# Key and query projections of a transformer layer by seven half-size products in place of eight, with modulation columns moved to other stages

## The chip, the cores and the metric

The kernel runs on one core of a Trainium2 chip. The metric is device time in microseconds for one execution of the whole program; the time of a kernel is the median of several runs. The profile shows one execution, with five engines: TensorE (PE, with its weight loads shown apart as PEld), VectorE (DVE), ScalarE (ACT), GpSimd (POOL) and SyncE (SP), which here only issues DMAs.

## The reference

One encoder layer, on 512 tokens of 1024 features in float32. Every token-wise product is followed by a gated addition to the residual stream `x`.

```python
mod = silu(c) @ w_mod + b_mod                       # 9 x 1024 values
(sh1, sc1, g1, sh2, sc2, g2, sh3, sc3, g3) = split(mod)

h = modulate(rmsnorm(x, norm_ffn1), sh1, sc1)
x = x + 0.5 * g1 * swiglu(h, w_ffn1_in, w_ffn1_out) # hidden width 2816

h = modulate(rmsnorm(x, norm_mix), sh2, sc2)        # one h for both mixers
qa, ka, va, qb, kb, vb, ga, gb = split(h @ w_in)
qa, ka = rope(rmsnorm(qa)), rope(rmsnorm(ka))       # 8 and 2 heads of 64
ya = window_gqa_sink(qa, ka, va, sink) @ w_branch_a # attention A, |i-j| <= 128
qb, kb = rope(rmsnorm(qb)), rope(rmsnorm(kb))       # 4 heads x 2 maps of 64, 512 columns each
ob = diff_attention(qb, kb, vb, lam)                # attention B, dense; vb 512 columns
yb = (rmsnorm(ob, subln) * 0.8) @ w_branch_b
x = x + g2 * ((sigmoid(ga) * ya + sigmoid(gb) * yb) @ w_out)

h = modulate(rmsnorm(x, norm_ffn2), sh3, sc3)
x = x + 0.5 * g3 * swiglu(h, w_ffn2_in, w_ffn2_out)
```

## The kernel before

**High and low parts.** Every fp32 operand of a matmul is split into two fp32r parts: `high`, a cast on ScalarE, and `low`, the difference, on VectorE (`split_from`, line 190). A product of two operands is three matmuls: high by high, high by low, low by high (`mm3`, lines 174 to 176). Weights arrive in a `raw`, `u` or `b` tile through SP's DMA queue and are split into one of five `high`/`low` slots (`high_low`). There are three loaders: `load_split` (cast on ScalarE, low part on VectorE), `load_halves` (the same in two halves), and `load_main`, which makes the low part without VectorE: ScalarE writes the negated high part as `low` in two passes (line 1134) and an accumulating DMA from POOL's queue adds the weight to it (line 1135).

**Stages in order.** First SwiGLU (0 to about 340 us of the profile), the boundary in which the norm and `h` for the mixers are made (`boundary`, `hidden`, lines 354 to 363) beside three gate products, projections of values, keys and queries of attention B (`project`, lines 1202 to 1204), two more gate products, projections for attention A (`project_pairs`, lines 1222 to 1224), attention B, attention A, the two branches (`branch`), the output product, the second SwiGLU.

**Seven products for eight.** In both SwiGLUs a 2 x 2 block product of weights and activations is made by seven block products (`Unit`): the sums of weight blocks are formed in place by accumulating DMAs on POOL's queue (line 513), the sums of activation blocks by `h_sum` on VectorE, and the products are combined in `after` on VectorE (lines 538, 543, 546) and copied on ScalarE (line 536). A `Unit` names its products s1, a11, a12, s2, s4, s3 and a22; each has 24 matmuls of 256 columns at a depth of four blocks of 128 (`two`, lines 458 to 460). `ASK` and `MAKE` say how many products ahead a weight is loaded and split. The PSUM banks are x (a11, s2, s3, a22), v (s1, s4) and w (a12). `run_items` goes through a list of products, in order.

The projections of keys and queries don't use this before the change: each is four blocks of 128 tokens x 8 blocks of 128 features x 3 matmuls of 512 columns, with the activations as the stationary operand.

**Modulation columns.** The nine vectors of `mod` (G1, SC2, SH2, G2, SC3, SH3, G3 after the first two) are made 128 values at a time: a load of 512 KB of `w_mod` (line 245) and a pass of VectorE with an accumulator (`mod_col`, line 283). `column` works through lists of them: 24 in `rest`, beside the first SwiGLU (`side1`, with a credit of `SIDE` for each product), 24 in `later`, beside the value, key and query projections and two gates (`beside`, one for every `LATER` steps), and eight in `latest`, beside the output product. Columns of `later` are loaded into small `u` tiles.

**Order of the work.** In the SwiGLUs the order of instructions on SP and POOL is the program's; at the boundaries that of PE, VectorE and ScalarE. Between the value projection and the end of the branches a scheduler orders each engine's queue by its own estimate, by priority and readiness, and a planner (`Line`) puts pieces of the two attentions among the gate products and projections: each piece has a due time, worked out from estimated costs (`line.helped`), and conditions. Keys and queries are copied (`raws`), normed and rotated (`head_stats`, `rope`, lines 1256 to 1274 and 1317, with a power on POOL at line 1261), turned by four PE transposes a block (`turn_heads`, line 1281), and split. Gate products fill PE until attention B is done, the rest of them and the first branch while attention A goes on.

## Time and profile before

| what | us |
|---|---|
| median of three runs | 1034.86 (1034.34 to 1039.34) |
| the profiled execution, its own time | 1034.51 |
| its span, first to last instruction | 1032.7 |
| PE busy / VectorE / ScalarE / POOL | 1027.6 / 787.4 / 582.1 / 161.8 |

The granted clock is 0.999 of full speed over the whole span. PE's busy time counts modelled ends of overlapping matmuls, so what a matmul costs is read from the distance between two starts. An engine's idle time matters only where PE waits for it. A timeline row gives start and duration in us, the engine, the line, the operation, output and inputs; a row of groups gives count, busy us and mean ns, then the idle time ahead of the group.

### The profile page before, as it was taken

To read this page: it belongs to the slowest core of one execution; us is meant where nothing else is said; L and a number is where in the kernel's file an instruction comes from. 1 tells how busy PE (TensorE), PEld (TensorE's weight loads), DVE (VectorE), ACT (ScalarE), POOL (GpSimd) and SP (SyncE) were. 2 spreads that over 40 slices of the span, in tenths; PEclk is the share of its full clock that TensorE was granted. 3 is DMA by queue.
4 is the path that set the end of the run, shared out by engine and by line. 5 is a ranking of instruction groups with operands and counts; after the bars stand their busy time and mean duration, and the time that the engine had idled before them with its cause. 6 is when DMAs were issued, how large, how long until landed. Compare 5 with 4: busy or idle time off the path is not lost.

```text
span 1032.7 us, 18848 instructions
## 1 busy us (share of the span) xinstructions
PE 1027.6 (100%) x7346; PEld 949.0 (92%) x7346; DVE 787.4 (76%) x1457; ACT 582.1 (56%) x1013; POOL 161.8 (16%) x189
## 2 busy tenths in 40 slices
PE   9999999999999999999999999999999999999998
PEld 7889899899998998899888888989999999999998
DVE  7886667567787679859772588976898777877877
ACT  6755335244454443668785856525877556655553
POOL 1101110110100100543323101001112112212210
PEclk9999999999999999999999999999999999999999
DMA  9977887967875459796737944974498998989974
GB/s 363 371 207 202 239 241 219 251 153 243 218 188 158 144 213 410 237 281 135 181 79 185 259 136 151 367 250 103 93 239 195 238 236 209 222 228 215 207 158 113
DMA packets 70233, 220.39 MB, mean 213 GB/s; under 512 B 8448, under 2 KB 13184, under 8 KB 70144
## 3 DMA queue, kind: packets, MB, share of 16 engines
q1 hardware_dynamic: 47808, 146.52, 39.2%
q0 software_dynamic: 19200, 68.17, 35.9%
q10 hardware_dynamic: 3136, 4.51, 1.2%
q8 instruction: 57, 0.93, 0.4%
q14 instruction: 32, 0.26, 0.1%
HBM read 208.94 MB, written 10.23 MB: 212 GB/s over the span
## 4 chain that ended last, share of the span: by engine, by line
PE 96%; DVE 2%; ACT 2%; issue 0%; POOL 0%; DVEq 0%; ACTq 0%
PE acc L460 7%; PE acc L459 7%; PE acc L458 7%; PE sc L460 6%; PE sc L458 6%; PE sc L459 6%; PE sc L174 5%; PE sc L176 5%; PE sc L175 5%; PE acc L174 5%; PE acc L176 5%; PE acc L175 5%; PE tp L1281 2%; PE acc L709 2%; PE acc L1203 2%; PE acc L1202 2%
## 5 line engine op out<-in xcount | busy, mean ns | idle before, releaser
L190 ACT CAST high<-raw 128x1024 fp32r<-128x1024 f32 (+2 forms) x176 | 158.4, 914 | 149.4 <-PE sc L175 40.8
L190 DVE TENSOR_TENSOR low<-raw,high 128x1024 fp32r<-128x1024 f32 (+2 forms) x176 | 183.5, 1052 | 40.4 <-ACT high L190 38.8
L459 PE MATMUL acc<-b,high 128*128 128x256 f32 x508 | 140.5, 277 | 0.1
L458 PE MATMUL acc<-b,high 128*128 128x256 f32 x508 | 140.6, 277 | 0.0
L460 PE MATMUL acc<-b,low 128*128 128x256 f32 x508 | 140.5, 277 | 0.0
L460 PE MATMUL sc<-b,low 128*128 128x256 f32 x500 | 138.0, 276 | 0.0
L458 PE MATMUL sc<-b,high 128*128 128x256 f32 x500 | 138.0, 276 | 0.0
L459 PE MATMUL sc<-b,high 128*128 128x256 f32 x500 | 138.0, 276 | 0.0
L190 ACT CAST high<-u 128x1024 fp32r<-128x1024 f32 (+1 forms) x73 | 75.4, 1034 | 52.3 <-PE sc L175 20.0
L190 DVE TENSOR_TENSOR low<-u,high 128x1024 fp32r<-128x1024 f32 (+1 forms) x73 | 87.7, 1201 | 21.5 <-ACT high L190 20.0
L174 PE MATMUL sc<-b,high 128*128 128x512 f32 (+1 forms) x272 | 97.4, 358 | 0.0
L175 PE MATMUL sc<-b,high 128*128 128x512 f32 (+1 forms) x272 | 97.0, 357 | 0.0
L176 PE MATMUL sc<-b,low 128*128 128x512 f32 (+1 forms) x272 | 97.0, 357 | 0.0
L459 PEld LDWEIGHTS acc<-b,high 128*128 128x128 f32 x508 | 95.4, 188 | 0.5 <-DVE b L1903 0.3
L458 PEld LDWEIGHTS acc<-b,high 128*128 128x128 f32 x508 | 95.4, 188 | 0.2
L460 PEld LDWEIGHTS acc<-b,low 128*128 128x128 f32 x508 | 95.4, 188 | 0.1
L460 PEld LDWEIGHTS sc<-b,low 128*128 128x128 f32 x500 | 93.9, 188 | 0.0
L458 PEld LDWEIGHTS sc<-b,high 128*128 128x128 f32 x500 | 93.9, 188 | 0.0
L459 PEld LDWEIGHTS sc<-b,high 128*128 128x128 f32 x500 | 93.9, 188 | 0.0
L174 PE MATMUL acc<-b,high 128*128 128x512 f32 (+1 forms) x240 | 89.2, 372 | 0.0
L176 PE MATMUL acc<-b,low 128*128 128x512 f32 (+1 forms) x240 | 86.6, 361 | 0.0
L175 PE MATMUL acc<-b,high 128*128 128x512 f32 (+1 forms) x240 | 86.5, 360 | 0.0
(400 smaller groups left out, 2717.9 us busy)
## 6 DMA issues: line engine op xcount, KB each, us to landing
u<-w_mod SPq DMA_DIRECT2D x38, 512.0 KB, 8.0
b<-w_mod SPq DMA_DIRECT2D x32, 512.0 KB, 5.5
raw<-w2i SPq DMA_DIRECT2D x31, 512.0 KB, 5.6
u<-w2i POOLq DMA_DIRECT2D x31, 512.0 KB, 6.8
raw<-w1u SPq DMA_DIRECT2D x24, 512.0 KB, 6.5
u<-w1u POOLq DMA_DIRECT2D x24, 512.0 KB, 7.1
raw<-w1o SPq DMA_DIRECT2D x24, 384.0 KB, 4.8
raw<-w_gate SPq DMA_DIRECT2D x16, 512.0 KB, 5.4
```

Of the source, the lines that this page charges most:

```text
L174: PE.matmul(out, wh, xh, start=first, stop=False)
L175: PE.matmul(out, wh, xl, start=False, stop=False)
L176: PE.matmul(out, wl, xh, start=False, stop=last)
L190: last = S.copy(hi, src), V.tensor_tensor(lo, src, f(hi), ALU.subtract)
L458: PE.matmul(out, wh[:, s], xh, start=first and j == 0, stop=False, skip_group_check=True)
L459: PE.matmul(out, wh[:, s], xl, start=False, stop=False, skip_group_check=True)
L460: PE.matmul(out, wl[:, s], xh, start=False, stop=last and j == 1, skip_group_check=True)
L709: PE.matmul(out1[i][:, r], w[:, i * P : (i + 1) * P], h[:, r], start=first and r.start == 0, stop=last and r.stop == T, skip_group_check=True,
L1202: PE.matmul(out[t][:, 0:n], hh[k][:, ht], wh[:, o : o + n], start=k == 0, stop=False)
L1203: PE.matmul(out[t][:, 0:n], hh[k][:, ht], wl[:, o : o + n], start=False, stop=False)
L1281: PE.transpose(tp[:, j * P : (j + 1) * P], src, ident)
```

## The change

1. **Keys and queries by seven products.** `project` is left for the values only. `projected` makes a `Unit` for the keys and one for the queries, with `two_turned`: activations stationary, 256 columns of weights moving. The boundary's `hidden` writes, as one more ScalarE activation for each block and half, the fp32 value of `h`, of which `h_sum` makes four sums after the boundary, beside the value projection. `after` combines under a high priority. Each unit yields four quarters (256 tokens x 256 columns), which are normed and rotated by `two_blocks`, the helper of attention A, and turned four blocks at once. `item_steps` gives the planner a step for every six matmuls; the last query product a22 follows s3, with the load of gate 3 put ahead.
2. **Columns.** `rest` has 30 (credit 0.36, none at some of the last items), `later` 5 beside the value, key and query projections, and a new list `tail` 13, from the end of attention B's turns on, one for every third step of the gate products, in `u` tiles, each load after a gate's load in SP's queue. For them `silu(c)` is loaded again into a `raw` tile.
3. **The first branch's weights** are loaded by `load_split` in place of `load_main`.

The core of the diff:

```diff
-EARLY, NEXT, SIDE, LATER = 3, 3, 0.27, 4
+FIRST_BLOCK, BESIDE_V, SIDE, LATER = 30, 5, 0.36, (6, 14, 2)
...
         if value is not None:
...
-            S.activation(value, t3, AF.Identity, bias=s)
+            S.activation(value, t, AF.Identity, bias=s)
...
-                h = hidden(rs, c, sc, sh, hh[c], hl[c], r)
+                value = hq[f"b{c // 4 + 1}{n}"][:, c % 4 * H : (c % 4 + 1) * H]
+                h = hidden(rs, c, sc, sh, hh[c], hl[c], r, value)
...
+    def two_turned(po, w, k, x, first, last, js=range(2)):
+        (wh, wl), (xh, xl) = w, x
+        s = slice(k * 2 * P, (k + 1) * 2 * P)
+        for j in js:
+            r = slice(j * P, (j + 1) * P)
+            out = po[:, j * H : (j + 1) * H]
+            PE.matmul(out, xh[:, r], wh[:, s], start=first and j == 0, stop=False, skip_group_check=True)
+            PE.matmul(out, xl[:, r], wh[:, s], start=False, stop=False, skip_group_check=True)
+            PE.matmul(out, xh[:, r], wl[:, s], start=False, stop=last and j == 1, skip_group_check=True)
...
+    at = FIRST_BLOCK, FIRST_BLOCK + BESIDE_V, 6 * NC
+    rest, later, tail, latest = rest[: at[0]], rest[at[0] : at[1]], rest[at[1] : at[2]], rest[at[2] :]
...
+    def projected(w, post, odd):
+        u = Unit([w[i] for i in range(4)], 4, h1_operand, post, odd)
+        u.srcs = dict(zip(("a11", "a12", "a21", "a22"), u.srcs))
+        u.products, u.aside, u.urgent = two_turned, -ASIDE, True
+        u.in_order = ("s1", "s2", "s3", "s4", "a22")
+        return u
...
+    def keys_b(c, v, u):
+        n, i, raw = quarter(c, v)
+        rs = small(8)
+        y = two_blocks(raw, 4, table["kb"], i, rs.rearrange("p (t h) -> p t h", t=2), False)
+        y3 = y.rearrange("p (h d) -> p h d", d=HD)
+        V.tensor_tensor(y3, y3, rs.unsqueeze(2).broadcast_to([P, 8, HD]), ALU.mult)
+        def turn():
+            turn_quarter(y, n, i, kb_h, kb_l)
+            keys_done.add((n, i))
+        line.at(line.helped(3.2, 5.0) + SLACK, turn, ("tp",))
...
-        yield from beside(project(vb_w, T, values_b), LATER)
-        yield from beside(project(a["w_kb"], T, keys_b), LATER)
-        yield from beside(project(a["w_qb"], T, queries_b), LATER)
-        yield from beside(gates(lambda: gate_next[0] < EARLY_A), 1)
+            with tc.issue_after(split[0]), tc.issue_after(split[1]):
+                k.prepare("s1")
+            h_sum("n1", False)
+            for t in ("n2", "t3", "t4"):
+                h_sum(t, False)
...
+            yield from beside(project(vb_w, T, values_b, also), LATER[0])
+            items = [(k, p, None, None) for p in ("s1", "a11", "a12", "s2", "s4", "s3")]
+            items += [(q, "s1", None, None), (k, "a22", None, None)]
+            items += [(q, p, None, None) for p in ("a11", "a12", "s2", "s4")]
+            items += [(q, "s3", None, lambda: soon_gates.update({3: load_main(a["w_gate"][3], holder=3)})), (q, "a22", None, None)]
+            yield from beside(item_steps(items, MM3), LATER[1])
+            yield from beside(gates(lambda: gate_next[0] < EARLY_A), LATER[2])
...
-        yield from gates(lambda: done["b"] < NT)
+        place = sbuf("raw", [P, 1024], F32, RAW)
+        def ended():
+            if turns["b"] == 4 * NT and cact[0] is not place:
+                cact[0] = place
+                with tc.issue_after(loaded[0]):
+                    nc.sync.dma_start(place, c_scr.partition_broadcast(P))
+            return turns["b"] == 4 * NT
+        yield from beside(gates(lambda: done["b"] < NT), 3, tail, ended)
         line.drain(lambda: done["b"] == NT)
         start_a()
-        yield from gates()
+        yield from beside(gates(), 3, tail, ended)
+        while tail or asked:
+            column(tail)
...
-        yield from branch(a["w_yb"], 8, ob_h, ob_l, then_a, load_main)
+        yield from branch(a["w_yb"], 8, ob_h, ob_l, then_a, load_split)
```

More of the change, by code (lines that the diff above doesn't have):

```diff
@@ L530, in after, with combine @@
         def after(self, q):
+            self.done.add(q)
+            with tc.high_priority() if self.urgent else nullcontext():
+                rest = list(self.combine(q))
+            for c, v in rest:
+                self.post(c, v, self)
+        def combine(self, q):
             v, b = self.v, self.bank
-            self.done.add(q)
             if q in ("a11", "s1", "s2"):
@@ L575, in run_items @@
                 also()
-            u.multiply(q, ks)
+            if cost is None:
+                u.multiply(q, ks)
+                yield
+            else:
+                for k in range(u.depth):
+                    u.multiply(q, [k])
+                    yield cost
             if ks is None or u.depth - 1 in ks:
@@ L600, in h_operand, with h_sum @@
         return t[:, k, T1], t[:, k, T2]
-    def h_sum(t):
+    def h_sum(t, spare=True):
         p, q = SUMS[t]
         hq[t] = hq[q if t in ("t3", "t4") else p]
-        h_op[t] = [u4() for _ in range(2)] if t == "n1" else b8()
+        spare = spare and t == "n1"
+        h_op[t] = [u4() for _ in range(2)] if spare else b8()
         for i in range(2):
@@ L955, in item1 @@
     def item1(u, q, ks=None):
-        items1.append((u, q, ks, side1))
-    credit, asked = [0.0], []
+        pause = ks is not None if isinstance(u, Out1) else u.p == NH - 1 and q in ("s3", "s4", "a22")
+        items1.append((u, q, ks, lambda: side1(0.0 if pause else SIDE)))
+    credit, asked, summed, loaded = [0.0], [], [], []
     room = b8(F32).rearrange("p a b -> p (a b)")
@@ L1226, in project_pairs, with beside @@
         then(out)
-    gate_next = [3]
-    def beside(steps, every, columns=later):
-        for i, cost in enumerate(steps):
-            if (columns or asked) and i % every == every - 1:
+    gate_next, soon_gates = [3], {}
+    def beside(steps, every, columns=later, when=lambda: True):
+        i = 0
+        for cost in steps:
+            i += when()
+            if (columns or asked) and i % every == every - 1 and when():
                 column(columns)
@@ L1335, in values_b, with queries_b, turn @@
             line.helped(0.6)
-    def queries_b(ps):
-        queries(ps, table["qb"], rqb, qb_h, qb_l, lambda: diff_scores(0, 0))
-        for t in range(NT):
-            V.tensor_scalar(nrqb[:, t, :], rqb[:, t, :], -1.0, None, ALU.mult)
+    def queries_b(c, v, u):
+        n, i, raw = quarter(c, v)
+        rs = rqb[:, 2 * i : 2 * i + 2, 4 * n : 4 * n + 4]
+        y = two_blocks(raw, 4, table["qb"], i, rs, True)
+        V.tensor_scalar(nrqb[:, 2 * i : 2 * i + 2, 4 * n : 4 * n + 4], rs, -1.0, None, ALU.mult)
+        def turn():
+            turn_quarter(y, n, i, qb_h, qb_l)
+            queries_done.add((n, i))
+            if (n, i) == (0, 0):
+                line.at(
+                    line.free["tp"] + SLACK, lambda: diff_scores(0, 0), SCORES + (lambda: len(keys_done) == 4,)
+                )
+        line.at(line.helped(2.6, 5.0) + SLACK, turn, ("tp",))
     head_b = {}
```

146 lines of the change are left out of this document (66 added, 80 removed).

## The prediction

> **What bounds the kernel now.** I read the page first, then the waits of PE, then busy time by stage, then the single matmuls. Page, engines and the chain that ended last:
>
> ```profile
> span 1032.7 us, 18848 instructions
> PE 1027.6 (100%) x7346; PEld 949.0 (92%) x7346; DVE 787.4 (76%) x1457; ACT 582.1 (56%) x1013; POOL 161.8 (16%) x189
> PE 96%; DVE 2%; ACT 2%; issue 0%; POOL 0%; DVEq 0%; ACTq 0%
> ```
>
> All waits of PE that the profile names:
>
> ```profile
> PE acc L634 <- DVE sm L640: 0.9, 1, 0.9
> PE acc L187 <- DVE u L190: 0.2, 1, 0.2
> ```
>
> TensorE is the bound, and nothing waits in front of it: 1.1 us in all. So the kernel's time is the sum of the matmuls' spacings, and a change is worth what it takes out of that sum less the waits that it makes. What the other engines have free is read by stage (columns: length; busy us and count of PE, PEld, DVE, ACT, POOL; clock; DMA share; GB/s):
>
> ```profile
> 75.00:316.00 241.00, 241.00 (x1717) 225.00 (x1717) 173.74 (x242) 106.91 (x140) 26.06 (x30) 1.00 0.78 213
> 346.00:374.00 28.00, 28.00 (x236) 27.83 (x235) 21.44 (x48) 15.95 (x29) 3.64 (x6) 1.00 0.18 58
> 374.00:396.00 22.00, 22.00 (x99) 18.20 (x98) 16.75 (x29) 4.97 (x10) 0.00 (x0) 1.00 1.01 389
> 396.00:418.00 22.00, 22.00 (x99) 18.23 (x98) 19.33 (x38) 7.93 (x16) 0.00 (x0) 1.00 1.03 409
> 418.00:440.00 22.00, 22.00 (x102) 18.18 (x102) 20.45 (x42) 15.55 (x30) 13.19 (x8) 1.00 0.65 199
> 545.00:570.00 25.00, 25.00 (x133) 21.04 (x132) 5.70 (x13) 12.85 (x30) 6.46 (x11) 1.00 0.79 197
> 570.00:640.00 70.00, 69.84 (x449) 59.12 (x448) 54.29 (x184) 49.72 (x125) 5.68 (x8) 1.00 0.61 182
> ```
>
> The rows are the first SwiGLU, the boundary to the mixers, the projections of values, keys and queries (22 us each), the end of attention B, and attention A. VectorE is nearly full in the three projections and nearly idle at the end of B.
>
> **The products.** Spacing of one projection matmul today, 512 columns wide: 13 steps from the first row to the last.
>
> ```profile
> 395.85 0.39 PE L1204 MATMUL acc<-high,b 128*128 128x512 f32 x1
> ...
> 398.79 0.39 PE L1202 MATMUL acc<-high,b 128*128 128x512 f32 x1
> ```
>
> 2.94 / 13 = 0.226 us. Keys and queries are 2 x 4 blocks x 8 k x 3 = 192 of them: 43.5 us. Seven products of 4 k x 2 halves x 3 make 168 matmuls per projection, 336 in all, each 256 wide. What does one cost? Four stretches of 256-wide matmuls, first and last row of each:
>
> ```profile
> 369.77 0.28 PE L175 MATMUL acc<-b,u 128*128 128x256 f32 x1
> ...
> 373.49 0.28 PE L176 MATMUL acc<-b,u 128*128 128x256 f32 x1
> ...
> 451.27 0.28 PE L1222 MATMUL acc<-high,b 128*128 128x256 f32 x1
> ...
> 456.99 0.28 PE L1223 MATMUL acc<-low,b 128*128 128x256 f32 x1
> ...
> 488.05 0.28 PE L1223 MATMUL acc<-low,b 128*128 128x256 f32 x1
> ...
> 488.84 0.28 PE L1224 MATMUL acc<-high,b 128*128 128x256 f32 x1
> ...
> 899.73 0.28 PE L459 MATMUL sc<-b,high 128*128 128x256 f32 x1
> ...
> 901.89 0.28 PE L460 MATMUL sc<-b,low 128*128 128x256 f32 x1
> ```
>
> 31 steps of 0.120 (weights in a u tile), 49 of 0.117 and 7 of 0.113 (attention A's projections, with activations as the stationary operand, the form the change uses), 19 of 0.114 (second SwiGLU). So 336 of them cost 38.0 to 40.3 us; I take the middle of the two A rows, 0.115, the nearest form: 38.6 us. The gain is 43.5 - 38.6 = 4.9 us, between 3.2 and 5.5. Sixteen transposes per projection stay sixteen.
>
> The Trainium skill, TensorE: Matmul & The Clock Gate, section Back-to-back issue gap, speaks against this: in streams of weight load and matmul it gives about 81 ns at 128 columns and 131 ns at 512, so half the width would cost clearly more than half. By that rule, interpolated (an estimate), 256 columns cost about three quarters of 512 and the change would lose some 14 us. The rows above show half, 0.115 against 0.226, and they decide.
>
> **What is added on VectorE and ScalarE.** Mean durations (busy us, mean ns):
>
> ```profile
> L190 DVE TENSOR_TENSOR low<-raw,high 128x1024 fp32r<-128x1024 f32 x104 | 126.5, 1223 | 28.8 <-ACT high L190 27.2
> L283 DVE CUSTOM_DVE_ANT_0 u<-u,ka,begin 128x1024 f32<-128x1024 f32 x8 | 10.3, 1283 | 6.1 <-DMA u<-w_mod 4.5 <-PE sc L1203 1.6
> L190 DVE TENSOR_TENSOR b<-f,b 128x512 fp32r<-128x512 f32 x22 | 15.1, 689 | 5.7 <-ACT b L190 5.7
> L1273 DVE TENSOR_TENSOR f<-f,raw 128x256 f32<-128x256 f32 x16 | 6.2, 421 | 0.0
> L355 ACT ACTIVATE b<-f,mod 128x256 fp32r<-128x256 f32 x16 | 7.9, 507 | 4.9 <-DVE f L354 4.9
> L1261 POOL TENSOR_TENSOR sm<-sm,half 128x8 f32<-128x8 f32 x4 | 9.9, 2482 | 61.1 <-DVE sm L1260 61.1
> u<-w2i POOLq DMA_DIRECT2D x31, 512.0 KB, 6.8
> ```
>
> *Boundary.* Sixteen more activations (the fp32 value of each half of h): 16 x 0.51 = 8.1 us on ScalarE, which goes from 16 to 24 of 28 us. The last low part of h comes at
>
> ```profile
> 367.53 0.48 DVE L363 SCALAR_TENSOR_TENSOR b<-f,mod,b 128x256 fp32r<-128x256 f32 x1 [0.18 <-ACT b L355]
> ```
>
> and PE needs it nine gate matmuls before 373.49 + 0.12, at about 372.5: 4.5 us of slack. A lateness of 1 to 2 us is hidden; the cover gone, it would cost what exceeds 4.5. Taken as 0.1 (bounds 0 and 2).
>
> *Value projection (22 us).* VectorE gets four sums (8 subtractions, 8 low parts, 16 x 0.69 = 11.0), three weight splits (3.7), five columns (6.4); with the values' four low parts (2.8) 24 us by row means. Queue starts lie about 0.08 closer than durations, so it just fits; only the first sum is needed when keys begin. Cost 0 (bound 1).
>
> *Keys and queries.* Eleven weight splits (13.5), six additions that combine products (4.1), and per quarter the norm and rotation: four or, for keys, five whole passes (the reduction, two products or sums, the keys' scaling, the low part after the turn) and two half ones, 4 x 0.69 + 2 x 0.42 = 3.6 or 4.3, in all 31.6. With the two late columns about 51 us against 38.6 us of products. Before it was 40 of 44, many of the moved columns among them. The excess of some 12 us spills over, as rotations can, into the next two gates (48 matmuls x 0.226 = 10.9 us of PE work that needs no VectorE). What cannot wait are the weights. A product's 24 matmuls last 2.8 us. From preparing s2 to using s4 there are five products, 13.8 us; the path is a cast and low part (2.3), an accumulating load (0.9 issue, perhaps behind a 2.5 us power on POOL, 6.8 to land), and a cast and low part again: 12.3 to 14.8. So it is just in time or about 1 us late, once per projection, and more if a rotation is ahead of it in VectorE's queue; gate 3, whose weights are loaded early, can be pulled forward. I take 1.2 us of waits in all (bounds 0 and 8.8, two waits of a whole quarter's rotation).
>
> *End of the queries.* The product a22 follows s3 in the same bank, so it must wait for VectorE's addition. The same order stands at the end of the first SwiGLU:
>
> ```profile
> 317.21 0.28 PE L460 MATMUL acc<-b,low 128*128 128x256 f32 x1
> ...
> 317.68 0.28 PE L174 MATMUL sc<-b,high 128*128 128x256 f32 x1
> 318.00 0.50 PE L174 MATMUL acc<-b,high 128*128 128x512 f32 x1
> 318.34 0.39 PE L175 MATMUL acc<-b,high 128*128 128x512 f32 x1
> 318.58 0.28 PE L458 MATMUL acc<-b,high 128*128 128x256 f32 x1
> ```
>
> There 1.37 us pass from s3's last to a22's first matmul, filled with other products but for about 0.3 us (the steps of 0.32 and 0.34 against 0.11 and 0.23). I take 0.3; bounds 0 and 1.3.
>
> **The moved columns.** Six go into the first SwiGLU: 7.7 us on a VectorE with 67 us free, 3 MB on queues at 78%: 0. Thirteen (16.7 us) go to the end of attention B, where VectorE has 19 of 25 us free; beside them the low parts of four branch tiles (4.9 us) enter attention A, where it has 16 of 70 free, while ScalarE loses two passes per tile and POOL's queue four accumulating loads. Their 13 loads stand on SP's queue among the gates': 6.8 MB on top of 197 GB/s x 25 us = 4.9 MB is 11.7 MB, 29 us at the 409 GB/s of the key stage. So loads can come late by some 3 us in all, ahead of gates that are fetched early: I take 0.2 (bounds 0 and 3). The earlier start of attention B that fewer columns allow is worth nothing by itself: matmuls of gates and branches fill all gaps already.
>
> **Sum.** -4.9 + 0.1 + 1.2 + 0.3 + 0.2 = -3.1 us. The profiled execution took 1034.51 us, its span 1032.7; the median shown is 1034.86, 0.35 above. 1034.51 - 3.1 = 1031.4 for a profiled execution; the products are regular work and I lean a little to less waiting, since nowhere else does this order of seven products show a wait: 1031.3 us.
>
> **Rivals.**
> *VectorE becomes the bound of keys and queries (slower).* If rotations stand ahead of weight splits in its queue and the gates are not pulled forward, PE takes VectorE's 51 us instead of 38.6: +12.4 - 4.9 = +7.5, 1042 us. For it: 20.45 of 22 us busy in the query stage already, POOL's power of 2.5 us in the same chain. Against: no wait of PE on a weight today. It decides from 4.9 us of waits on. The Trainium skill, SBUF — State Buffer, section Who interferes with whom, has VectorE and GpSimd share a port pair; that would lengthen POOL's part further, and no row here isolates it.
> *Weight loads set the pace (slower).*
>
> ```profile
> L1222 PEld LDWEIGHTS acc<-high,b 128*128 128x128 f32 x96 | 18.1, 188 | 0.8 <-issue 0.7
> ```
>
> Unhidden, 336 x 0.188 = 63.2 us, +19.7: 1054 us. The spacing of 0.115 in just these rows speaks against it.
> *The full gain.* 0.113 a matmul and no wait: -5.5, 1029.1 to 1029.4 us.
> *The gain is eaten.* 0.120 a matmul saves 3.2, and 2 to 4 us of waits take it: 1033.5 to 1035.5 us.
>
> **How the numbers follow.** A difference of 0.5%, 5.2 us, is about what a measurement of this kernel can tell from no change. Chances: the sum 0.53, the gain eaten 0.19, the full gain 0.14, VectorE the bound 0.12, weight loads 0.02. The full gain passes 1029.7 (half a per cent) in most of its cases: faster 0.13. Of VectorE as the bound, the worse part passes 1040: slower 0.11 with the weight loads. The rest, 0.76, is no change that can be told. The range 1029.0 to 1037.0 leaves out the worse part of the VectorE case, the weight loads and a little below.
>
> **What would show it.** Right: in the key and query stage 336 matmuls 256 wide at 0.113 to 0.117; fewer PE instructions of 512 columns by 192; VectorE near full there and busy at the end of B; PE still at 100% with waits under 3 us. Wrong: PE waits on low parts L190 or on the copies of the combined products, or on gate loads at the end of B; spacing of 0.12 and more; a gap before the first value matmul.

## The result, and the profile after

The changed kernel takes 1064.84 us (median of four, 1062.81 to 1069.71) against 1035.04 for the kernel before in the same session: a ratio of 1.0294, 95% interval 1.0276 to 1.0313. It is slower by 30 us; forecast were 1031.3 and a range of 1029.0 to 1037.0. The profiled execution took 1069.71, its span is 1067.9. The ratios leave out one execution, of the products alone (experiment 1), which took 1292 us at a granted clock of 0.75.

Page of the changed kernel: span, engines, and the chain that ended last, by engine.

```profile
span 1067.9 us, 19195 instructions
PE 1036.0 (97%) x7490; PEld 960.7 (90%) x7490; DVE 810.7 (76%) x1481; ACT 591.7 (55%) x1023; POOL 166.8 (16%) x193
PE 76%; DMA 8%; DVE 7%; ACT 5%; issue 3%; POOL 1%; ACTq 0%; DVEq 0%; POOLq 0%; SPq 0%
```

TensorE was 96% of that chain and is now 76%: it waits for others. Its largest waits (in all, times, longest):

```profile
PE tp L1303 <- DMA f<-qa_scr: 11.9, 1, 11.9
PE acc L176 <- DMA low<-w_gate: 4.2, 1, 4.2
PE acc L469 <- DVE low L190: 3.1, 2, 1.9
```

The stages that were shown of before, without the values, which stay full (length; busy us and count of PE, PEld, DVE, ACT, POOL; clock; DMA share; GB/s):

```profile
75.00:316.00 241.00, 240.19 (x1709) 224.03 (x1708) 177.60 (x249) 105.96 (x140) 26.03 (x30) 1.00 0.81 228
346.00:374.00 28.00, 27.73 (x234) 27.51 (x233) 21.52 (x52) 20.02 (x44) 3.64 (x6) 1.00 0.12 45
396.00:418.00 22.00, 21.28 (x174) 20.70 (x173) 17.02 (x27) 10.92 (x14) 4.43 (x4) 1.00 0.73 137
418.00:440.00 22.00, 17.23 (x143) 16.48 (x142) 18.55 (x35) 13.07 (x22) 11.34 (x6) 1.00 0.36 90
545.00:570.00 25.00, 25.00 (x125) 20.69 (x124) 9.08 (x24) 12.48 (x29) 7.81 (x11) 1.00 1.05 304
570.00:640.00 70.00, 57.15 (x348) 46.96 (x348) 49.22 (x146) 38.41 (x91) 1.75 (x2) 0.90 0.65 212
```

Two stages lose: keys and queries (PE 17.23 of 22 us), and the start of attention A (57.15 of 70, at a granted clock of 0.90). The products themselves cost what was said. First and last of 27 matmuls of the new form:

```profile
398.77 0.28 PE L468 MATMUL sc<-high,b 128*128 128x256 f32 x1
...
401.82 0.28 PE L467 MATMUL sc<-high,b 128*128 128x256 f32 x1
```

3.05 / 26 = 0.117 us (forecast 0.115).

Where the 35.2 us between the two profiled spans (1067.9 and 1032.7) stand can be counted by the distances of matmul starts above the plain ones, 0.227 us for 512 columns and 0.113 for 256, in both traces: some 16 to 17 more from 396 to 500, of which about 7 belong to gate 3's load and the slow clock behind it; some 14 from 545 to 640; 4 in a slower stretch of the second SwiGLU (last section); 6 spread over the rest. The products' shorter work takes off 4.9.

**The largest loss.** TensorE, then SyncE's queue, at the end of attention B:

```profile
569.89 0.39 PE L176 MATMUL acc<-b,low 128*128 128x512 f32 x1
582.21 1.09 PE L1303 MATMUL tp<-ident,f 128*128 128x128 f32 x4 [11.93 <-DMA f<-qa_scr]
...
583.52 0.63 PE L175 MATMUL acc<-b,high 128*128 128x512 f32 x1
583.94 0.63 PE L176 MATMUL acc<-b,low 128*128 128x512 f32 x1
```

```profile
542.84 2.99 SPq L245 DMA_DIRECT2D u<-w_mod  x4
547.84 0.33 SPq L1160 DMA_DIRECT2D raw<-w_gate  x1
551.30 2.02 SPq L245 DMA_DIRECT2D u<-w_mod  x3
555.44 0.33 SPq L1575 DMA_DIRECT2D u<-mask  x1
555.92 13.28 SPq L245 DMA_DIRECT2D u<-w_mod  x3
571.46 0.33 SPq L1570 DMA_DIRECT2D f<-qa_scr  x1
```

The transposes that open attention A wait 12 us for their first queries. These are fetched by an issue at 571.46, behind ten loads of moved columns that wait, one after another, for a free `u` tile. In the kernel before the same fetch was issued at 540.1. Behind the wait a 512-column matmul takes 0.42 us instead of 0.227 for some 4 us: the granted clock is 0.50 from 580 to 586. The fetch is not the only thing that moved: counted in both traces from 340 us on, the kernel before puts 48 more gate matmuls of 512 columns ahead of these transposes, two gate products or 10.9 us. So in the changed kernel less work covers a late fetch.

**The second.** Gate 3's accumulating load (issue on GpSimd's queue, and TensorE):

```profile
436.69 1.74 POOL L1529 TENSOR_TENSOR rqb<-rqb,half 128x8 f32<-128x8 f32 x1 [5.28 <-DVE rqb L1526]
438.62 0.92 POOL L1167 DMA_DIRECT2D low<-w_gate  x1 [0.19 <-issue]
```

```profile
447.72 0.76 PE L176 MATMUL acc<-b,low 128*128 128x512 f32 x1 [4.22 <-DMA low<-w_gate]
448.28 0.41 PE L467 MATMUL acc<-high,b 128*128 128x256 f32 x1
448.50 0.41 PE L468 MATMUL acc<-high,b 128*128 128x256 f32 x1
```

The issue stands behind a query quarter's power, which waited 5.28 us for VectorE. TensorE loses 4.2 us, then half of its clock for the last query product (0.22 us a matmul instead of 0.114).

### The profile page after: what moved, and what is told of

Same layout as the page of the kernel before. It is cut to its first block, busy times and chain, and to the rows that moved or that the text cites. A ratio compares the mean times of both kernels' runs of the same rounds, so it can differ in the third digit from the quotient of the medians.

```text
span 1067.9 us, 19195 instructions
## 1 busy us (share of the span) xinstructions
PE 1036.0 (97%) x7490; PEld 960.7 (90%) x7490; DVE 810.7 (76%) x1481; ACT 591.7 (55%) x1023; POOL 166.8 (16%) x193
## 4 chain that ended last, share of the span: by engine, by line
PE 76%; DMA 8%; DVE 7%; ACT 5%; issue 3%; POOL 1%; ACTq 0%; DVEq 0%; POOLq 0%; SPq 0%
PE sc L456 6%; PE sc L457 6%; PE sc L458 6%; PE acc L456 5%; PE acc L457 5%; PE acc L458 5%; PE sc L174 5%; PE sc L175 5%; PE sc L176 5%; PE acc L174 3%; PE acc L176 3%; PE acc L175 3%; DMA u<-w_mod 2%; DMA u<-w2o 2%; PE acc L736 2%
## 5 line engine op out<-in xcount | busy, mean ns | idle before, releaser
L190 ACT CAST high<-raw 128x1024 fp32r<-128x1024 f32 (+2 forms) x172 | 162.0, 950 | 156.7 <-PE sc L175 45.0
L190 DVE TENSOR_TENSOR low<-raw,high 128x1024 fp32r<-128x1024 f32 (+2 forms) x172 | 187.4, 1096 | 36.4 <-ACT high L190 35.2
L190 ACT CAST high<-u 128x1024 fp32r<-128x1024 f32 (+1 forms) x76 | 78.5, 1034 | 60.4 <-PE sc L175 18.7
L190 DVE TENSOR_TENSOR low<-u,high 128x1024 fp32r<-128x1024 f32 (+1 forms) x76 | 91.2, 1201 | 24.1 <-ACT high L190 22.2
```

The lines of the kernel that those rows point to most:

```text
L190: last = S.copy(hi, src), V.tensor_tensor(lo, src, f(hi), ALU.subtract)
```

## The experiments

Each ratio is to the kernel before, run beside it. The theory at first: the loads at the end of B, and VectorE in keys and queries, are two separate losses. The rivals: only one of them counts, or the order of the attentions does.

**1. The two parts of the change, each alone.** Columns and branch as in the change, with the old products:

```diff
-EARLY, NEXT, SIDE, LATER = 3, 3, 0.27, 4      # kernel before
+FIRST_BLOCK, BESIDE_V, SIDE, LATER = 30, 5, 0.36, (6, 6, 2)
+        yield from beside(gates(lambda: done["b"] < NT), 3, tail, ended)
```

> The kernel before (1034.9 us) with the columns moved as in the change (30 in the first SwiGLU, 5 beside the values, 13 from the end of attention B on) and the low parts of the first branch on VectorE, but with the eight full products and the old rotation of keys and queries. Theory, the columns at the end of B make the largest loss by themselves: a wait of 10 to 13 us for attention A's queries and about 2 us of lowered clock, 1047 to 1050 us, less up to 2 where fewer columns stand beside keys and queries. Rival, the wait comes from the products' reordering (B ends at another place among the gates): 1033 to 1037 us.

1049.8 us, 1.0138 (1.0120 to 1.0156): the columns alone cost 15 us. The number is the theory's, the path to it mostly is not. Ten column loads stand ahead of the fetch here too, and it goes out at 564.3, 24 us later than in the kernel before, yet the wait that was to be 10 to 13 us is 2.2:

```profile
PE tp L1288 <- DMA f<-qa_scr: 2.2, 1, 2.2
```

In this run the 48 gate matmuls still lie ahead of the transposes, so most of the lateness is covered: to that extent the rival, that the wait comes from the products' reordering, is right. By the distances of matmul starts, against the kernel before, 8 us are lost from 545 to 700, the fetch among them, 4 in the slower stretch of the second SwiGLU, and some 3 in small waits elsewhere. That the sum came to 15 was luck. And the new products with the old lists:

```diff
-FIRST_BLOCK, BESIDE_V, SIDE, LATER = 30, 5, 0.36, (6, 14, 2)   # changed kernel
+FIRST_BLOCK, BESIDE_V, SIDE, LATER = 24, 24, 0.27, (4, 4, 1)
-        ... then_a, load_split)
+        ... then_a, load_main)
```

> The changed kernel with the columns where the kernel before has them (24 in the first SwiGLU, 24 beside values, keys and queries, none from the end of attention B on) and the first branch's low parts by accumulating loads as before: of the change, the seven products and the new rotation stay alone. Columns alone cost 15 us (1049.8). Theory, the products have a loss of their own from 396 to 470 (12 to 14 us of waits and lowered clock), and 19 more columns on VectorE (24 us) there add to it, while the end of B is free: 1055 to 1065 us. Rival, without tail columns the products are nearly harmless: 1040 us or less.

1.0357 (1.0336 to 1.0378), about 1072 us: +37, more than the theory's 1065 and far from the rival. Its waits and its stage of keys and queries, 396 to 470:

```profile
PE tp L1303 <- DVE mod L294: 7.1, 3, 5.3
PE sc L467 <- ACT f L552: 5.5, 1, 5.5
PE acc L469 <- DVE low L190: 4.8, 3, 2.8
```

```profile
396.00:470.00 74.00, 55.60 (x392) 51.87 (x390) 58.71 (x110) 25.84 (x40) 23.27 (x13) 0.88 0.74 217
```

No fetch wait is left there. Most of the named waits are on VectorE's queue, where column sums stand ahead of what TensorE needs, but not all: the one of 5.5 us is for a copy that stands in ScalarE's queue behind a cast, and the cast waits for a query weight that lands late, while seven column loads are issued between 390 and 403.

```profile
409.12 1.05 ACT L190 CAST high<-u 128x1024 fp32r<-128x1024 f32 x1 [8.95 <-DMA u<-w_qb]
```

So 15 and 37 give 30 together: each part costs by itself, and moving the columns takes back about 22 us of what the products lose with the old lists.

**2. Is it the order of SyncE's queue, or the bytes?** Columns not begun before the fetch, in the text:

```diff
-        yield from beside(gates(lambda: done["b"] < NT), 3, tail, ended)
+        yield from gates(lambda: done["b"] < NT)
```

> The changed kernel (1064.8 us) without column loads ahead of attention A's fetches: the gates at the end of attention B are run plainly, and all 13 columns go beside the gates that follow the fetches. Theory, order of SyncE's queue: in the changed kernel TensorE stands 12.3 us (569.9 to 582.2) for the fetch of attention A's queries, which is issued at 571.46 behind 11 column loads that wait for free tiles; with them behind, the fetch is issued at about 540, the wait goes to under 1 us and with it some 2 us of lowered clock: 1050 to 1052 us, and up to 2 more if the columns now disturb attention A. Rival, the DMA queues are full at the end of B whatever the order (share 1.05): gates' loads alone keep the fetch late, the wait stays over 6 us and the time is 1058 or more.

1056.4 us, 1.0204 (1.0185 to 1.0222). In between: the scheduler still put five column loads ahead of the fetch, which went out at 552.9, 18.6 us earlier; 2.8 us of the wait stayed. Then the fetch on another queue:

```diff
-        nc.sync.dma_start(ys[0], qa_scr[order[0]])
+        G.dma_start(ys[0], qa_scr[order[0]])      # and the values, the other three, the mask
```

> The changed kernel with the fetches of attention A's queries, values and mask issued on GpSimd's queue and not on SyncE's; the 13 columns stay at the end of attention B with all their bytes. Theory, order of the queue: the fetch no longer stands behind the column loads' waits for tiles, the 12.3 us wait falls to 0 to 3 us (landing times of 5 to 12 us in a full stretch): 1050 to 1055 us. Rival, bytes: the loads share the same 16 engines, which are at 1.05 there with column loads landing 5 to 21 us after issue, so the fetch still lands 8 us or more late: 1060 us or more.

1064.3 us, 1.0282 (1.0259 to 1.0305): nothing won; the rival's number. Issued at 560.8, 11 us earlier than in the changed kernel, the fetch took longer to land; its wait fell to 5.3 us, and a wait of 4.3 us on VectorE came in attention A. The same columns with a sixteenth of their bytes (the rest of these sums is left out):

```diff
-                asked.append((v, c, mod_load(v, c, w)))
+                nc.sync.dma_start(w[:, 0:64], a["w_mod"][v * NC + c][:, 0:64])   # tail only
+                asked.append((v, c, w[:, 0:64]))
```

> The changed kernel in which each of the 13 columns from attention B's end on loads and sums only its first 64 of 1024 elements (32 KB for 512); their places in the order of all queues are kept, the rest of these sums is left out. Columns alone cost 15 us, and moving the fetch of A's queries to another queue changed nothing, so theory: it is their bytes, 6.8 MB in a stretch whose queues are at 1.05, that make both the free tiles and the fetch late; the 12.3 us wait falls to under 2 us and its lowered clock goes: 1048 to 1053 us. Rival, the order of SyncE's queue and its waits for free tiles, whatever the size of a load: a wait of over 8 us stays, 1060 us or more.

1049.4 us, 1.0137 (1.0110 to 1.0164), as the theory of the bytes has it. Loads around the fetch (KB each, median us from issue to landing): first the changed kernel, then the fetch on GpSimd's queue, then without the bytes.

```profile
u<-w_mod SPq DMA_DIRECT2D x13, 512.0 KB, 12.5
low<-w_gate POOLq DMA_DIRECT2D x7, 512.0 KB, 11.1
```

```profile
f<-qa_scr POOLq DMA_DIRECT2D x4, 256.0 KB, 15.4
```

```profile
f<-qa_scr SPq DMA_DIRECT2D x4, 256.0 KB, 6.6
u<-w_mod SPq DMA_DIRECT2D x6, 32.0 KB, 3.1
```

With the bytes, a fetch of 256 KB needs 15 us on GpSimd's queue; without them 6.6 on SyncE's, and the first is issued at 560.52 though the same ten column loads stand ahead of it. So bytes and order act together: a slow landing keeps the `u` tile, the next load waits for the tile, and the fetch waits behind it. Attention A then runs full:

```profile
570.00:640.00 70.00, 69.19 (x440) 57.60 (x438) 53.14 (x189) 42.56 (x105) 1.34 (x2) 1.00 0.49 150
```

(These 13 short sums also spare VectorE some 15 us, in a stretch where it is busy 9 of 25 us; that part isn't separated. In the two profiled executions 11.5 of the 16.7 us between the spans stand from 545 to 640, and almost 4 in the slower stretch of the second SwiGLU, which the run without the bytes doesn't have.)

**3. Can the columns stand elsewhere?** Tied behind the last fetch:

```diff
-            with tc.issue_after(loaded[0]) if columns is tail else nullcontext():
+            with tc.issue_after(banded_last[0]) if columns is tail else nullcontext():
```

> As the run without columns ahead of the fetch (1056.4 us), but each of the 13 column loads is now tied behind the last of attention A's fetches: in that run five column loads still went out at 542 to 552, before the first fetch at 552.89, because the order of SyncE's queue is not the order of the text there. Theory, column loads and the late write are both in it: the fetch now waits only for the queries' own write (issued at 541 to 544, against 507 in the kernel before) and goes out at about 550, the 3.2 us wait and the 5 us of half clock behind it go: 1049 to 1052 us. Rival, the write of the rotated queries alone makes the fetch late: wait and time as before this edit, 1055 to 1058 us.

1076.5 us, 1.0385 (1.0354 to 1.0416). Both numbers missed. The fetch's wait is gone, as the theory says, and the next in line wait instead, the gates' low parts:

```profile
PE acc L176 <- DMA low<-w_gate: 15.8, 3, 5.8
```

All in the first SwiGLU:

```diff
-FIRST_BLOCK, BESIDE_V, SIDE, LATER = 30, 5, 0.36, (6, 14, 2)
+FIRST_BLOCK, BESIDE_V, SIDE, LATER = 43, 5, 0.52, (6, 14, 2)
```

> The changed kernel with 43 columns in the first SwiGLU, 5 beside the values and none at the end of attention B. Theory: with the 13 columns away the fetch of attention A's queries goes out as soon as they are written, about 552, and what is left of the 12.3 us wait is 0 to 2 us; the columns in attention A's gates no longer disturb it; the first SwiGLU takes 13 more columns (16.7 us of VectorE, 6.8 MB) for 0 to 2 us: 1046 to 1050 us. Rival, the first SwiGLU's DMA queues (share 0.81 with 30 columns) are overrun and its weights come late: 1055 us or more.

1066.3 us, 1.0304 (1.0288 to 1.0320): the rival's outcome. The wait for the fetch is away, but values begin 19 us later (394.8 against 375.8). With 30 columns values begin 2.2 us later than before the change, with 43 another 19; the DMA share of the stage goes only from 0.81 to 0.82. TensorE's own largest wait from 75 to 346 is on copies of ScalarE (3.5 us in three), but behind it stand loads. The chain that leads to the first of these waits, at 168.46, begins with a weight that lands 6.6 us after its issue (`raw<-w1u`, 158.74) and goes on through casts and the copy on ScalarE; and VectorE waits more than twice as long for columns, first with 43 of them, then with 30:

```profile
DVE b L283 <- DMA b<-w_mod: 14.2, 7, 3.3
```

```profile
DVE b L283 <- DMA b<-w_mod: 6.3, 3, 4.1
```

Half the clock follows here too (0.50 from 170 to 173), which adds to the 19 us.

Beside the branches (with B held back, see 4):

```diff
-        yield from branch(a["w_yb"], 8, ob_h, ob_l, then_a, load_split)
+        yield from beside(branch(a["w_yb"], 8, ob_h, ob_l, then_a, load_split), 3, tail)   # w_ya: 4
```

> Attention B held back as in that run (1055.7 us), and the 13 columns beside the three branches' products instead of from B's end on. Theory, what the columns cost is their 6.8 MB in a stretch that has none to spare, 540 to 640; after 640 the queues are at about 0.7 and VectorE is not full, so there they cost 0 to 2 us, and attention A loses its waits for the fetch: 1045 to 1050 us. Rival, a column hurts wherever it stands, as in the first SwiGLU (13 columns there cost some 17 us before the values begin): 1054 us or more.

1071.3 us, 1.0347 (1.0319 to 1.0374): the rival again. Attention A starts without a wait, and from 650 to 740 PE is busy 78.81 us of 90, where the changed kernel has 89.90. In none of the places that were tried did the 13 columns come near the 0.2 us of the sum.

**4. The order of the attentions.** B's first scores held until A's key products are through, as before the change:

```diff
-   SCORES + (lambda: len(keys_done) == 4,)
+   SCORES + (lambda: len(keys_done) == 4 and "k" in wa and keys_a_done,)
```

> The changed kernel, with attention B's first scores held back until the key products of attention A are through, which is the order that the kernel before has. Theory: in the changed kernel B's scores start 12 us earlier and A's projections end 35 us later (530 against 495), so A's last queries are written at 545 instead of 507, and VectorE has no room to catch up behind the queries of B. Held back, A's projections end by 505, the write is out by 520 and the waits of 440 to 470 shrink by 2 us; but the 11 column loads still stand ahead of the fetch on SyncE's queue, so that at most a third of the 12.3 us goes: 1057 to 1062 us. Rival, the late write is the cause of the 12.3 us: under 1053 us. Second rival, the order is of no matter: 1063 to 1066 us.

1055.7 us, 1.0200 (1.0185 to 1.0215), between theory and rival, and the best version of the change that computes everything. The fetch still goes out late, at 566.6, but B ends 17 us later (543 against 526), and the 48 gate matmuls that the changed kernel lacks ahead of the transposes are there again: these begin at 579.72 after a wait of 0.8 us. The order was worth 9 us, most of it by cover: TensorE comes to the transposes 9 us later, and the fetch lands 2.5 us earlier.

**5. Keys and queries.** Gate 3's low part without GpSimd:

```diff
-   load_main(a["w_gate"][3], holder=3)
+   load_split(a["w_gate"][3], holder=3)
```

> The changed kernel with the low part of gate 3's weights subtracted on VectorE instead of by an accumulating load on GpSimd's queue. Theory, GpSimd's queue: there the load stands behind a query quarter's power, which waits until 436.7 for VectorE, is issued at 438.62 and lands at 447.6, TensorE waits 4.6 us and then runs at half clock for about 2.4 us: without it 1057 to 1059 us. Rival, VectorE is the bound of this stage and the low part (1.22 us) only lengthens its queue: a wait of the same length on the low part, 1063 to 1066 us.

1063.2 us, 1.0277 (1.0258 to 1.0296): the rival. The 4.2 us are gone and B's first transposes wait 2.6 us for a low part on VectorE. Without the half products of the rotation:

```diff
+        if plain:            # keys and queries of B
+            return y
         for o, q in ((slice(0, NF), slice(NF, HD)), ...
```

> The changed kernel without the two half products with the sines and the addition in the rotation of attention B's keys and queries (8 quarters x 1.5 us of VectorE are left out). Theory, VectorE's queue is what the products of keys and queries wait for: the waits on low parts and copies between 411 and 440 (7 us) fall to 3 us or less, and gate 3's load, whose issue stands behind a query quarter's power that waits for VectorE, comes 1.5 to 3 us earlier: 1054 to 1060 us. Rival, the chain of a product's weights (cast, low part, accumulating load, cast, low part) is too long for the places where it is begun, whoever else uses VectorE: the waits of 425.0 and 437.6 stay, 1062 to 1066 us.

1063.8 us, 1.0274 (1.0259 to 1.0289): the rival's number, not for its reason. The waits of 425 and 437 on weights went, and a wait of 4.5 us on a quarter's low part came, of transposes. Twelve us of work less, and VectorE stands still instead (VectorE, then GpSimd):

```profile
421.20 0.69 DVE L1349 TENSOR_TENSOR f<-f,sm 128x512 f32<-128x512 f32 x1 [1.56 <-POOL sm L1529]
...
426.05 0.69 DVE L1349 TENSOR_TENSOR f<-f,sm 128x512 f32<-128x512 f32 x1 [1.75 <-POOL sm L1529]
```

```profile
418.53 2.63 POOL L1529 TENSOR_TENSOR sm<-sm,half 128x8 f32<-128x8 f32 x1
424.38 1.63 POOL L1529 TENSOR_TENSOR sm<-sm,half 128x8 f32<-128x8 f32 x1 [3.22 <-DVE sm L1528]
```

VectorE's queue is in order, and the keys' scaling waits in it for GpSimd's power. So that wait was taken away too:

```diff
-        V.tensor_tensor(y3, y3, rs..., ALU.mult)     # the keys' scaling
-        V.tensor_scalar(nrqb[...], rs, -1.0, None, ALU.mult)
         def turn():
+            V.tensor_scalar(nrqb[...], rs, -1.0, None, ALU.mult)
```

> The changed kernel without the half products and the addition of the rotation and without the keys' scaling by GpSimd's power (left out), and with the queries' negated norms formed at the transposes: in the run without rotation alone VectorE stood idle for GpSimd's power four times (1.6 to 1.8 us each), in order, so that nothing was won. Theory, VectorE's queue with its waits for GpSimd bounds keys and queries: with both gone the waits of 396 to 460 (14.7 us of spacing over the plain one) fall to 5 us or less: 1053 to 1057 us. Rival, the chain of the weights sets the pace: 10 us or more of them stay, 1060 us or more.

1058.8 us, 1.0212 (1.0183 to 1.0241), 6 us better than the changed kernel: between both. The stage too lies between theory (5 us or less of its waits left) and rival (10 or more): by the distances of matmul starts, against the kernel before, 7 of 15 us are left from 396 to 460. From 396 to 470, first the changed kernel, then this one:

```profile
396.00:470.00 74.00, 64.29 (x462) 58.89 (x461) 58.74 (x117) 44.66 (x80) 25.90 (x18) 0.95 0.72 174
```

```profile
396.00:470.00 74.00, 69.76 (x538) 64.24 (x538) 53.35 (x106) 52.35 (x96) 25.27 (x19) 1.00 0.78 198
```

5.5 us more of PE in the same time. So VectorE's queue with its waits for GpSimd makes about half of this loss; what makes the other half is not shown. Less work on VectorE by accumulating loads, with B held back:

```diff
-                split_from(hi, lo, t)
+                S.copy(hi, t); S.activation(lo, t, AF.Identity, scale=-1.0)   # a11, a12, a22
+                G.dma_start(lo, self.srcs[q], accum_op=ALU.add)
+        u.MAKE = dict(u.MAKE, a11=5, a12=4, a22=4)               # begun two products earlier
```

> Attention B held back (1055.7 us), and in both projections the low parts of a11, a12 and a22 no longer subtracted on VectorE (6 x 1.22 us) but made by a negated copy on ScalarE and an accumulating load, begun two products earlier. Theory, VectorE is the bound there and 7.3 us less work on it give back 3 to 6 us: 1050 to 1053 us. Rival, the accumulating loads stand on GpSimd's queue behind powers that wait for VectorE, as gate 3's does, and TensorE waits for them: 1056 to 1064 us.

1062.1 us, 1.0253 (1.0229 to 1.0276), 6 worse than its base: gate 3's load now makes TensorE wait 6.4 us and a query weight's 3.2, behind powers on GpSimd's queue, and a wait of 3.4 us for a copy of ScalarE is new. The rival.

**6. The branch's low parts.**

```diff
-   ob_h, ob_l, then_a, load_split)
+   ob_h, ob_l, then_a, load_main)
```

> The changed kernel with the first branch's low parts made by accumulating loads again, as in the kernel before: the last part of the change undone by itself. Theory, it is of no weight: VectorE has room in attention A, four loads more or fewer on GpSimd's queue change little: within 2 us of the changed kernel, 1062 to 1067 us. Rival, the 4.9 us on VectorE add to the columns there and make the 3 us of small waits of 600 to 650: 1060 us or less.

1062.1 us, 1.0256 (1.0230 to 1.0283): its interval overlaps the changed kernel's, so this part can't be told from nothing.

**7. Mended together.** 43 columns in the SwiGLU, B held, gate 3 on VectorE:

```diff
+FIRST_BLOCK, BESIDE_V, SIDE, LATER = 43, 5, 0.52, (6, 14, 2)
+   SCORES + (lambda: len(keys_done) == 4 and "k" in wa and keys_a_done,)
+   soon_gates.update({3: load_split(a["w_gate"][3], holder=3)})
```

> Three edits in one: 43 columns in the first SwiGLU and none at B's end, attention B held back until A's key products are through, gate 3's low part on VectorE. Theory, the three losses are separate and what is left are the waits on VectorE inside keys and queries (7 us) and some at values (2 us), against 4.9 us gained by the products: 1036 to 1041 us. Rival, VectorE is the bound from 396 to 470 and each edit only moves its wait to the next reader: 1044 to 1049 us.

1061.7 us, 1.0261 (1.0246 to 1.0277): both missed, since the SwiGLU took the gain. B held, columns beside the branches, and three edits in keys and queries:

```diff
+        u.MAKE = dict(u.MAKE, a12=3, s3=3)
+   load_main(a["w_gate"][3], spare=True)      # at the query's a11, in u tiles
-   line.at(line.helped(2.6, 5.0) + SLACK, turn, ("tp",))
+   line.at(line.helped(2.6, 8.0) + SLACK, turn, ("tp",))     # keys alike
```

> That kernel (B held back, columns beside the branches) with three more edits in keys and queries: the weights of a12 and s3 are prepared three products ahead instead of two; gate 3's weights are loaded ten products' quarters earlier, into tiles of their own, so that their accumulating load stands ahead of the queries' powers on GpSimd's queue; and the quarters' transposes stand 3 us later in TensorE's order. Theory, these are waits for things that begin too late: of the 12 to 14 us between 411 and 450 at most 5 are left, 1036 to 1042 us. Rival, VectorE's work there is more than the time, so that an earlier start of one only delays the other: 1044 us or more.

1069.7 us, 1.0330 (1.0307 to 1.0352), 1.5 under its base, which its interval can't tell from nothing: the rival. Starting earlier on the same VectorE is worth little. Last, the columns without bytes and the lighter rotation, both diffs above in one kernel:

> The changed kernel with both of those edits at once: the columns from B's end on load and sum 64 of 1024 elements, and the rotation of B's keys and queries is without half products, addition and the keys' scaling (left out). Alone they gave 15.4 and 6.0 us. Theory, the two losses are separate places and add: 1042 to 1046 us, and what then stands above the 1030 that the products alone would give are gate 3's load, waits of the boundary and of attention A. Rival, with the wait for the fetch gone the later stages take the lateness up or give it back: under 1040 or over 1048 us.

1043.2 us, 1.0081 (1.0064 to 1.0098). 15.4 and 6.0 alone, 21.6 together: they add. And with three diffs above as well, B held, gate 3's `load_main` at a11 and the branch by loads:

> That kernel, and with it attention B held back until A's key products are through, gate 3's weights loaded before the queries' powers into tiles of their own, and the first branch's low parts by accumulating loads. Theory, these take the 4 us of gate 3 with its lowered clock and 1 to 2 us in attention A: 1036 to 1040 us, still not below the kernel before. Rival, gate 3's earlier load takes a place on ScalarE and GpSimd from the queries and the gain is lost: 1042 us or more.

1046.7 us, 1.0114 (1.0099 to 1.0129): the rival; once the fetch is in time the three together cost 3.5 us. No version came below the kernel before.

## Why the prediction was wrong

The step that failed first is the term for the 13 loads on SyncE's queue, 0.2 (bounds 0 and 3). In the changed kernel it is 15 us: that much goes when their bytes are taken away, and with it the wait of 11.9 us. The bytes were worked out rightly as more than the stretch holds (29 us for 25), but the 3 to 4 us of excess was taken as the whole cost. What was left out is who stands behind: attention A's fetch, in the same queue, behind loads that wait for tiles; then the 12 us wait halves the clock. That gates are fetched early protected the gates; the fetch wasn't named. The run of the columns alone also costs 15 us, but doesn't show this path: its wait for the fetch is 2.2 us. The 11.9 need the late fetch and the lost cover together (third step below).

The second is "weights late in keys and queries, 1.2 (bounds 0 and 8.8)", with its spill "as rotations can, into the next two gates". It is about 16 us from 396 to 500, 7 of them gate 3's. VectorE is busy as long as before (58.74 and 58.26 us from 396 to 470), yet PE falls from 74.00 to 64.29: the weights of the next product and the rotations share one queue in order, so rotations stood ahead, with waits for GpSimd in them, and did not spill into the gates. Gate 3's load, which the prediction used as cover ("can be pulled forward"), was itself late by 4.2 us, since its issue stood behind a power on GpSimd's queue. The rival "VectorE becomes the bound" named this mechanism, with +7.5 us and a chance of 0.12: for the part that is shown it was the nearest, but by the order of the queue and not by a full engine, since VectorE is busy 58.74 of 74 us. Taking away the rotation's extra work with its wait for GpSimd gave 6.0, taking away the extra work alone nothing. It decides from 4.9 us of waits on, and these were passed.

The third is "the earlier start of attention B is worth nothing by itself". It cost about 9 us in the changed kernel (experiment 4), since two gate products that would have covered the fetch are used up before.

Right were the products' price (0.117 and 0.114 against 0.115), so the 4.9 us stand in the matmuls' own spacing, though no version kept them, and no slowing by weight loads. Six more columns in the first SwiGLU and the boundary, 0 and 0.1 in the sum, were small but not free: values begin 2.2 us later, and 0.7 in the columns' run. The 0.3 for the end of the queries can't be read by itself, since the wait for gate 3's load stands there.

Still open: of the 12.7 us between 1043.2 and the 1030.5 (1035.4 - 4.9) that the products alone should give, about 10 show, by the distances of matmul starts against the kernel before, from 396 to 500, 1 at the end of the first SwiGLU, and the rest behind 545. They weren't taken apart. And 13 columns at the end of B with all their bytes but another tile ring weren't tried.

## What to carry to other kernels

Price a moved transfer by what stands behind it in its queue, not by its bytes alone: find the next transfer that the critical engine needs there, ask when its issue comes if each load ahead must first wait for a tile, and count the work that the critical engine has until then (here two gate products decided between a wait of 2.2 and one of 11.9 us). Equal busy time of a helper engine doesn't mean equal cost: what was slack work there can become part of the chain when short products wait for the same in-order queue, and a wait for a third engine inside that queue counts as work. When a change frees one stage and fills another, run both halves alone first: here 37 and 15 against 30 show in two runs that the halves don't add. And look at the waits of such a run, not only at its time: the 15 fitted the expectation, its path did not.

## What was not expected of the hardware

**Half clock after a wait.** After waits of 11.93 and 4.22 us TensorE ran at half speed for some 4 and 5.5 us: 512 columns in 0.42 us for 0.227, 256 in 0.21 for 0.114. So a wait cost 2 to 2.7 us more than its length. After the named wait of 1.9 us that ends at 439.82 it did not slow down. The length alone doesn't decide it, though. In the run of experiment 6 half speed followed a wait of 1.85 us and not one of 2.73; the two waits, then the granted clock (behind PE's busy time and count) behind each:

```profile
438.35 0.38 PE L469 MATMUL acc<-low,b 128*128 128x256 f32 x1 [1.85 <-DVE low L190]
446.37 0.47 PE L176 MATMUL acc<-b,low 128*128 128x512 f32 x1 [2.73 <-DMA low<-w_gate]
```

```profile
440.00:442.00 2.00, 2.00 (x11) 0.50 0.91 139
448.00:450.00 2.00, 2.00 (x18) 1.00 1.03 369
```

The Trainium skill, TensorE: Matmul & The Clock Gate, section Part 1: The HAM clock gate, says that the clock falls to 4/8 after an idle window of about 3.4 us. The two long waits agree with it; the wait of 1.85 us, and one of 1.82 with 43 columns in the first SwiGLU, do not, and here the measurement decides.

**GpSimd's power and VectorE.** The power of 128x8 took 1.63 us where VectorE stood still (424.38 above) and 2.63 where it worked at first (418.53); 1.66 to 3.30 in the changed kernel. The Trainium skill, SBUF — State Buffer, section Who interferes with whom, has a VectorE instruction with two SBUF inputs contend with a GpSimd instruction that reads SBUF. These rows fit it, though no run isolates it.

**A slower stretch without a wait.** In the profiled execution of the changed kernel some 108 us of the second SwiGLU, from 848.9 to 956.9, run at 0.118 us a matmul instead of 0.113, at a granted clock of 1.00, which costs 4.1 us. PE alone, 850 to 950, in the changed kernel and then in the one with B held:

```profile
850.00:950.00 100.00, 100.00 (x851) 1.00 0.87 209
```

```profile
850.00:950.00 100.00, 100.00 (x884) 1.00 0.90 221
```

The run of the columns alone has such a stretch too (829.3 to 937.2), again 108 us long, the others don't have it in that place. It may be behind much of the 7 us between executions of the changed kernel; its cause was not found.
